# Splitting twelve unsplit float32 weight units: high part and negative by ScalarE, the rest by an adding transfer

## The chip, the cores and the metric

One core of a Trainium2 chip runs the kernel. The metric is the device time of one execution in microseconds; the median of several runs is what versions are compared by. Engines: PE (TensorE, matrix products; PEld are its weight loads), DVE (VectorE), ACT (ScalarE), POOL (GpSimd) and SP (SyncE, which here issues the loads). They run in parallel, each in the order of its own program, and wait for each other by semaphores.

## What is computed

Two transformer blocks in float32 on 256 tokens of width 1024. The first has sparse attention, retention and a gated feed-forward layer. The second has two layers, each of this form, and it is here that the change lies:

```python
h = rmsnorm(x, norm1_g[l])
u = h @ w_in[l]                       # q, k, v (512 each), 1024 for the convolution branch, 512 for the Fourier branch
y_a = differential_attention(q, k, v) @ w_proj_a[l]
cv = depthwise_conv(ga * sigmoid(gb), 31 taps) + conv_b[l]
y_b = silu(layernorm(cv)) @ w_proj_b[l]
y_c = fft2(four_in).real @ w_proj_c[l]
gates = sigmoid(h @ w_gate[l] + b_gate[l])      # three gates of 1024
merged = gates[0] * y_a + gates[1] * y_b + gates[2] * y_c
x = x + merged @ w_out[l]
x = x + (silu(f_gate) * f_up) @ w_ffn_out[l]    # f_gate, f_up = rmsnorm(x) @ w_ffn_in[l]
```

## The kernel before, in words

**Weights.** All weights come from HBM in 414 units, in the order of their use, each mostly 128 x 1024 float32 (512 KB). A unit is loaded by SP into one of `STAGE` = 5 staging buffers (`fetch`). For nearly all of them `split` then makes two parts in the reduced format float32r: ACT writes the high part `whi` (a conversion), DVE the low part `wlo` = weight - high part (`low`, one call later). There are `RING` = 8 buffers of each; a unit may be split when the unit eight before it is done. A product with a split weight is three products (`mm3`): high x high, high x low, low x high, as the activations are kept in two such parts too.

**The twelve others.** In each of the second block's layers the last two of the four units of the value projection (weight columns 1024 to 1535) and the last four of the eight units of the third gate (gate 2) are of the kind `WHOLE`. They are not split: PE multiplies the staged float32 weight with float32 activations (`self.whole`) in one float32 product each. Such a unit takes no slot of the ring, and keeps its staging buffer until its last product is done. `norm_steps(whole=True)` writes `self.whole` by four ACT copies at the end of the norm ahead of the layer (line 526).

**Ticks.** The program calls `tick` after each unit's products (for the projections of 512 columns after blocks of four or eight). A tick runs one step of every job that follows from the products just issued (jobs of priority 0: copies, gates, and the attention's steps), then `advance` (low parts, loads, and the split of one unit, or of two if under six units stand ready), then jobs of priority 1 to 3. The order of instructions on each engine is thus fixed when the program is written out.

**Order of a layer (`mix2`).** q, the convolution branch's inputs, k, the Fourier input, the value projection, gate 2, branch c, gate 0, gate 1, branch a (four units), branch b (four units), then w_out. Branch b multiplies the convolution's result, `slot[0]`.

**The convolution** (`convolve`, priority 3) is 124 DVE steps per layer (31 taps x 4 blocks) that are dealt out by credit, and `conv_norm` behind them, one stage for each tick: mean (PE) and subtraction (DVE); square (ACT); variance (PE), copy (DVE) and root (POOL); transposes (PE) and product (DVE); silu (ACT); high part (ACT); low part (DVE). Whatever is left of it is issued by `finish(conv)` right before branch b. `spent` is what an engine's instructions are planned to take:

```python
def vector_cost(name, out, args):
    return 0.065 + _width(args[0] if name == "tensor_reduce" else out) / 960
def tensor_cost(name, out, args):
    passes = 4 if args[0].dtype == F32 and name == "matmul" else 1
    return max(_width(out) * passes, 128) / 2400
...
while credit < 0.4 and not pace["last"]:
    mark = v.spent, t.spent
    yield
    credit += (t.spent - mark[1]) * pace["conv"] - (v.spent - mark[0])
credit -= 0.4
```

`pace["conv"]` is 1.0 from the value projection on.

Of the kernel before, what the change touches and what calls it, by code (L numbers as in the profile page):

```python
# [13 lines left out]
ALU = mybir.AluOpType  # L14
# [8 lines left out]
NF = FF // 128  # L23
LEAD_PAIRS = 2
CMP_AT = 9
WHOLE = 2
HEAD_ORDER = [g * 4 + p for p in range(4) for g in range(2)]


# [28 lines left out]
    return out + _pairs(w, FF)[2 * LEAD_PAIRS:]  # L58


WHOLES = {1024: 2, 0: 4}


def _whole(units, c):

    n = WHOLES.get(c, 0)
    return units[:len(units) - n] + [(t, WHOLE) for t, _ in units[len(units) - n:]]


def weight_units(a):  # L70
    out = []
    w = a["w_in"][0]
    heads = w[:, :512].reshape(D, 8, 64)[:, HEAD_ORDER].reshape(D, 512)
    kv = w[:, 512:1280].reshape(D, 6, 128)
    gates = w[:, 1280:1304].reshape(D, 8, 3)[:, HEAD_ORDER].reshape(D, 24)
    out += _token_major(np.concatenate([kv[:, 2], kv[:, 4], kv[:, 0], kv[:, 1]], 1))
    out += _token_major(heads)
    out += _token_major(np.concatenate([kv[:, 3], kv[:, 5], gates], 1))
    ret = [t for c in range(1304, 3352, 512) for t in _token_major(w[:, c:c + 512])]
    merge = _feature_major(w[:, 4376:6424])  # L80
    cmp = [(t, 1) for n in ("cmp_w1_k", "cmp_w1_v") for t, _ in _token_major(a[n][0], 4)]
    lin = out + ret
    out = []
    for i in range(len(lin)):
        out += lin[i:i + 1] + cmp[i - CMP_AT:i - CMP_AT + 1] * (CMP_AT <= i < CMP_AT + 8)
    out += merge[:8]
    for c in (3352, 3864):
        out += _token_major(w[:, c:c + 512])
    out += merge[8:]
    out += _feature_major(a["w_ret_branch"][0])  # L90
    out += _feature_major(a["w_nsa_branch"][0].reshape(8, 64, D)[HEAD_ORDER].reshape(512, D))
    out += _token_major(a["w_mix_out"][0], 1)
    out += _ffn_up(a["w_ffn_up"][0])
    out += _token_major(a["w_ffn_down"][0], 1)
    for l in range(2):
        w = a["w_in_2"][l]
        out += _token_major(w[:, :512])
        out += _pairs(w[:, 1536:2560], 512)
        for c in (512, 2560, 1024):
            out += _whole(_token_major(w[:, c:c + 512]), c)  # L100
        gate = [_feature_major(a["w_gate_2"][l][:, i * D:(i + 1) * D]) for i in range(3)]
        proj = [_feature_major(a[f"w_proj_{n}_2"][l]) for n in "abc"]
        out += _whole(gate[2], 0) + proj[2] + gate[0] + gate[1] + proj[0] + proj[1]
        out += _token_major(a["w_out_2"][l], 1)
        out += _ffn_up(a["w_ffn_in_2"][l])
        out += _token_major(a["w_ffn_out_2"][l], 1)
    return out
# [158 lines left out]
class Body:  # L266
# [3 lines left out]
    def __init__(self, ctx, tc, units, coff, poff, x, wts, cst, prm, rows, out):  # L270
        self.ctx, self.tc, self.nc = ctx, tc, Engines(tc.nc)
        self.units, self.coff, self.poff = units, coff, poff
        self.xin, self.wts, self.cst, self.prm, self.rows, self.out = x, wts, cst, prm, rows, out
        self.n = 0
        self.bg = []
        self.pending = None
        self.norming = None
        self.offs = np.concatenate([[0], np.cumsum([128 * u[0] for u in units])])
        self.fetched = self.split_to = 0
        self.look = self.STAGE  # L280
        self.raws, self.open, self.lows, self.held = {}, [], [], []
        self.ready, self.taken = ([], []), ([], [])

    def nm(self, s):
# [23 lines left out]
    def fetch(self):  # L308
        while (self.fetched < min(len(self.units), self.split_to + self.look)
               and (len(self.open) < self.STAGE or self.open[-self.STAGE][1])):  # L310
            i = self.fetched
            self.fetched += 1
            e = self.raws[i] = self.stage()
            w = self.units[i][0]
            self.nc.sync.dma_start(e[0][:, :w], bass.AP(tensor=self.wts.tensor,
                                                        offset=self.wts.offset + int(self.offs[i]), ap=[[w, 128], [1, w]]))

    def low(self):
        for hi, lo, e, w in self.lows:
# [4 lines left out]
    def split(self):  # L324
        i = self.split_to
        n = len(self.held)
        if i == len(self.units):
            return False
        w, kind = self.units[i]
        if kind != WHOLE and n >= self.RING and not self.held[n - self.RING][2]:  # L330
            return False
        self.fetch()
        if i not in self.raws:
            return False
        e = self.raws.pop(i)
        self.split_to += 1
        if kind == WHOLE:
            self.ready[0].append([e[0][:, :w], None, e])
            return True
        hi = self.t(self.wp, [128, 1024], "whi", F32R, bufs=self.RING)[:, :w]  # L340
        lo = self.t(self.wp, [128, 1024], "wlo", F32R, bufs=self.RING)[:, :w]
        self.nc.scalar.activation(hi, e[0][:, :w], AF.Copy)  # L342
        self.lows.append((hi, lo, e, w))
        u = [hi, lo, False]
        self.held.append(u)
        self.ready[kind].append(u)
        return True

    def advance(self):
        self.low()  # L350
        self.fetch()
        behind = sum(len(r) for r in self.ready) < 6 and self.norming is None
        for _ in range(2 if behind else 1):
            if not self.split():
                return

    def take(self, kind=0):
# [3 lines left out]
        u = self.ready[kind].pop(0)  # L361
        if any(x[0] is u[0] for x in self.lows):
            self.low()
        self.taken[kind].append(u)
        return u[:2]

    def done(self, n=1, kind=0):

        for _ in range(n):
            u = self.taken[kind].pop(0)  # L370
            if u[1] is None:
                u[2][1] = True
            u[2] = True


    def tick(self):
# [89 lines left out]
        return lambda: self.hi(hi[d], pv, scale), lambda: self.lo(hi[d], lo[d], pv, scale), pv  # L466


    def norm_steps(self, g_fin=None, whole=False):
        nc = self.nc  # L470
        stt, act = nc.vector.scalar_tensor_tensor, nc.scalar.activation
        if whole:
            self.whole = self.t(self.ap_, [128, KD, S], "act", bufs=4)
        acts = self.acts = self.act()
        rest = []
        g, pend = self.next_gain, self.pending
        es, rs = [None] * NT, {}
        half = [slice(i * 512, (i + 1) * 512) for i in range(2)]
# [42 lines left out]
                    stt(xs, xs, rs[tb][1][:, 0:1], g_fin[:, half[i]], op0=ALU.mult, op1=ALU.mult)  # L521

        def turn(tb, i):
            *fs, p = self.transpose4(es[tb][0], *acts, tb, 4 * i)
            if whole:
                rest.append(lambda: act(self.whole[:, 4 * i:4 * i + 4, tb * 128:tb * 128 + 128], p, AF.Copy))
            return fs

        add(0, 0)
        square(0, 0)  # L530
# [34 lines left out]
        for f in turn(1, 1):  # L565
            f()
        es[1][1] = True
        for f in rest:
            f()
        for tb in range(NT):  # L570
            final(tb)
        self.pending = None
# [9 lines left out]
    def lin_tok(self, n, consume, lead=False, tag="lin"):  # L582
# [4 lines left out]
        def block(todo):  # L587
            for i, (tb, k) in enumerate(todo):
                u = k // 2
                if u not in ws:  # L590
                    ws[u] = [w if w is None else w[:, :2 * n].rearrange("p (k n) -> p k n", k=2) for w in self.take()]
                wh, wl = ws[u]
                s = slice(tb * 128, (tb + 1) * 128)
                if wl is None:
                    self.nc.tensor.matmul(p[tb][:, :n], self.whole[:, k, s], wh[:, k % 2], start=k == 0, stop=k == KD - 1)
                else:
                    self.mm3(p[tb][:, :n], hi[:, k, s], lo[:, k, s], wh[:, k % 2], wl[:, k % 2], k == 0, k == KD - 1)
                if k == KD - 1:
                    consume(tb, p[tb][:, :n])
                if lead and i == 1 and (tb, k) == (0, 5):  # L600
# [19 lines left out]
    def lin_feat(self, acts, nk, groups, consume, start=0, tag="lin"):  # L620
        hi, lo = acts
        for g in range(start, groups):
            p = self.ps(tag).rearrange("p (f t) -> p f t", f=2)
            for f in range(2):
                if nk == KD or f == 0:
                    wh, wl = [w if w is None else w.rearrange("p (f k n) -> p f k n", k=nk, n=128) for w in self.take()]
                i = 0 if nk == KD else f
                for k in range(nk):
                    if wl is None:
                        self.nc.tensor.matmul(p[:, f], wh[:, i, k], self.whole[:, k], start=k == 0, stop=k == nk - 1)  # L630
                    else:
                        self.mm3(p[:, f], wh[:, i, k], wl[:, i, k], hi[:, k], lo[:, k], k == 0, k == nk - 1)
                if nk == KD or f == 1:
                    self.done()
                    if f == 1:
# [19 lines left out]
                    consume(g, ps)  # L655
                self.tick()

    def lin_res(self, acts, nk, g_fin=None, whole=False):
        hi, lo = acts
        final = self.next_gain is None  # L660
        cols = [[(0, 512), (512, 512)], [(0, 512), (512, 512)]]
# [37 lines left out]
                    self.tick()  # L699
            return  # L700
        self.pending = p
        self.norming = self.norm_steps(g_fin, whole)
        for tb in range(NT):
            for h in range(2):
                for kc in range(body, nk):
# [9 lines left out]
    def run(self):  # L715
# [65 lines left out]
        self.ffn(conv=True)  # L781
        for l in range(2):
            self.mix2(l)
            self.ffn(conv=False, whole=l == 0)

    def small_values(self):
        copy = self.nc.vector.tensor_copy
# [24 lines left out]
        yield  # L812


    def ffn(self, conv, whole=True):
        nc = self.nc
        stt, act = nc.vector.scalar_tensor_tensor, nc.scalar.activation
        with ExitStack() as ctx:
# [58 lines left out]
                self.lin_feat(self.acts, KD, NF, consume, start=LEAD_PAIRS, tag="s")  # L877
            else:
                self.lin_joint(self.acts, NF, consume_joint, start=LEAD_PAIRS)
            self.lin_res((hidh, hidl), NF, g_fin, whole)  # L880

    def lead_pairs(self, pool, consume):

# [876 lines left out]
```

## Time and profile before

| | |
|---|---|
| median of three runs | 1305.24 us (1305.23 to 1305.93) |
| the profiled execution | 1306.04 us |
| its span, first to last instruction | 1304.3 us |
| granted TensorE clock | 1.00 |
| PE busy | 1286.6 us (99%) |
| DVE, ACT, POOL busy | 923.2, 713.2, 68.9 us |
| loads and stores | 225.94 MB |

The profile is of one execution. Of its time 1.7 us lie around the span. Busy time is the union of an engine's instructions; the chain is the work that ended last, followed back from the last instruction to what released each step. Durations of single products are modelled to their ends, so the distance from one piece of the chain to the next is the better measure of what PE spends.

### The profile page before, as it was taken

What the parts mean: (1) busy time and instruction counts of PE and PEld (TensorE: products, weight loads), DVE (VectorE), ACT (ScalarE), POOL (GpSimd) and SP (SyncE); (2) the same over time, 40 slices, a digit from 0 to 9 for tenths busy, and PEclk for the clock granted to TensorE, in tenths of its full rate; (3) what the DMA queues carried; (4) which work ended last, traced back from release to release, by engine and by line L of the source; (5) the groups of instructions that cost most, each with busy time, mean ns of one, the idle gap of its engine ahead of it and who ended that gap; (6) DMA issues with size and microseconds to landing.
All of it is one profiled execution on the core that took longest, in us unless ns stands there. A gap on an engine that the chain in (4) does not pass through costs nothing.

```text
span 1304.3 us, 21120 instructions
## 1 busy us (share of the span) xinstructions
PE 1286.6 (99%) x8228; PEld 1149.1 (88%) x8228; DVE 923.2 (71%) x1521; ACT 713.2 (55%) x1259; POOL 68.9 (5%) x94
## 2 busy tenths in 40 slices
PE   6999999999999999999999999999999999999998
PEld 5878889999998879899998888888889999988887
DVE  5875555769887369998686766537989867766652
ACT  5664545457565364577455565436458664655540
POOL 0000000000000032100100000003100010000000
PEclk9999999999999999999999999999999999999999
DMA  8772235566566546245455655646525445565560
GB/s 294 263 239 97 82 129 184 186 195 201 176 191 208 163 139 216 99 146 172 155 178 190 196 182 188 205 142 199 188 74 183 159 145 178 195 193 188 183 195 33
DMA packets 63028, 225.94 MB, mean 173 GB/s; under 512 B 6992, under 2 KB 7376, under 8 KB 62928
## 3 DMA queue, kind: packets, MB, share of 16 engines
q1 hardware_dynamic: 62928, 224.60, 53.2%
q8 instruction: 64, 1.05, 0.3%
q14 instruction: 36, 0.29, 0.1%
HBM read 223.52 MB, written 1.05 MB: 172 GB/s over the span
## 4 chain that ended last, share of the span: by engine, by line
PE 95%; DVE 2%; DMA 1%; ACT 1%; issue 1%; POOL 0%; SPq 0%; POOLq 0%; ACTq 0%; DVEq 0%
PE lin L213 46%; PE s L213 38%; PE o L213 11%; DMA stage<-in_wts 1%; DVE wlo L213 0%; DVE stage L213 0%; DVE vr L213 0%; ACT whi L342 0%; DVE x L213 0%; ACT act L419 0%; POOL rs L503 0%; DVE prt L213 0%; POOL rs L506 0%; DVE act L213 0%; POOL rs L504 0%
## 5 line engine op out<-in xcount | busy, mean ns | idle before, releaser
L213 DVE TENSOR_TENSOR wlo<-stage,whi 128x1024 fp32r<-128x1024 f32 x402 | 479.5, 1215 | 109.9 <-ACT whi L342 109.6
L342 ACT ACTIVATE whi<-stage 128x1024 fp32r<-128x1024 f32 x402 | 412.4, 1053 | 132.3 <-PE o L213 57.9
L213 PE MATMUL s<-act,whi 128*128 128x256 f32 (+1 forms) x1600 | 367.0, 316 | 0.0
L213 PE MATMUL s<-act,wlo 128*128 128x256 f32 x1024 | 288.8, 282 | 0.0
L213 PEld LDWEIGHTS s<-act,whi 128*128 128x128 f32 x1600 | 263.9, 191 | 20.9
L213 PE MATMUL lin<-act,whi 128*128 128x256 f32 (+1 forms) x1344 | 281.9, 303 | 0.0
L213 PEld LDWEIGHTS lin<-act,whi 128*128 128x128 f32 x1344 | 215.5, 191 | 9.3
L213 PE MATMUL lin<-act,wlo 128*128 128x256 f32 x768 | 216.7, 282 | 0.0
L213 PE MATMUL lin<-whi,act 128*128 128x512 f32 (+2 forms) x736 | 213.8, 366 | 0.4 <-DVE prt L213 0.4
L213 PEld LDWEIGHTS s<-act,wlo 128*128 128x128 f32 x1024 | 195.2, 191 | 0.0
L213 PEld LDWEIGHTS lin<-whi,act 128*128 128x128 f32 x736 | 132.9, 190 | 21.9 <-DVE prt L213 0.8
L213 PEld LDWEIGHTS lin<-act,wlo 128*128 128x128 f32 x768 | 146.5, 191 | 0.0
L213 PE MATMUL lin<-wlo,act 128*128 128x512 f32 (+2 forms) x368 | 132.5, 360 | 0.3 <-DVE wlo L213 0.3
L213 DVE SCALAR_TENSOR_TENSOR cv<-gl,prm,cv 128x256 f32<-128x256 f32 x240 | 99.8, 477 | 0.0
L213 PEld LDWEIGHTS lin<-wlo,act 128*128 128x128 f32 x368 | 70.1, 190 | 10.2 <-DVE wlo L213 0.8
L832 ACT ACTIVATE y<-s 128x256 f32<-128x256 f32 x56 | 21.5, 383 | 64.6 <-PE s L213 64.6
L213 DVE SCALAR_TENSOR_TENSOR y<-s,prm,y 128x255 f32<-128x255 f32 x88 | 40.3, 480 | 16.9 <-ACT y L855 15.3
L213 PE MATMUL lin<-wlo,hidh 128*128 128x512 f32 x132 | 52.2, 395 | 0.0
L213 PE MATMUL lin<-whi,hidl 128*128 128x512 f32 x132 | 52.2, 395 | 0.0
L213 PE MATMUL lin<-whi,hidh 128*128 128x512 f32 x132 | 52.0, 394 | 0.0
L213 PE MATMUL o<-whi,hidh 128*128 128x512 f32 (+1 forms) x132 | 49.8, 377 | 0.0
L213 PE MATMUL o<-wlo,hidh 128*128 128x512 f32 (+1 forms) x132 | 49.6, 376 | 0.0
(285 smaller groups left out, 1558.4 us busy)
## 6 DMA issues: line engine op xcount, KB each, us to landing
stage<-in_wts SPq DMA_DIRECT2D x410, 512.0 KB, 4.2
gbc<-in_rows SPq DMA_DIRECT2D x7, 512.0 KB, 4.4
stage<-in_wts SPq DMA_DIRECT2D x4, 280.0 KB, 4.0
x<-in_x SPq DMA_DIRECT2D x4, 256.0 KB, 5.3
on<-in_cst SPq DMA_DIRECT2D x1, 896.0 KB, 7.0
out_dram<-x SPq DMA_DIRECT2D x3, 256.0 KB, 2.0
cst<-in_cst SPq DMA_DIRECT2D x1, 514.5 KB, 5.2
gbc<-in_rows SPq DMA_DIRECT2D x2, 256.0 KB, 6.4
```

The lines of the kernel that those rows point to most:

```text
L213: return f(out, *args, **kw)
L342: self.nc.scalar.activation(hi, e[0][:, :w], AF.Copy)
L832: act(sg[0][:, f], ps[f][:, 1], AF.Copy)
```

## The change

The twelve units get the kind `SUMMED` in place of `WHOLE`. ACT writes the high part as for every unit, and also the negative of it, by a second conversion of the staged weight with scale -1, into the buffer of the low part. The staging buffer is free after that. At the next `advance` POOL issues a transfer that reads the unit's weights from HBM again and adds them onto that buffer, which then holds weight - high part. DVE has no part in it. The products become `mm3`, the units take slots of the ring, and the unsplit activations with their four copies go.

```diff
+    def add_up(self):
+
+        for lo, i in self.sums:
+            self.nc.gpsimd.dma_start(out=lo, in_=self.unit(i), accum_op=ALU.add)
+        self.sums = []
...
-        if kind != WHOLE and n >= self.RING and not self.held[n - self.RING][2]:
+        if n >= self.RING and not self.held[n - self.RING][2]:
             return False
...
-        if kind == WHOLE:
-            self.ready[0].append([e[0][:, :w], None, e])
-            return True
         hi = self.t(self.wp, [128, 1024], "whi", F32R, bufs=self.RING)[:, :w]
         lo = self.t(self.wp, [128, 1024], "wlo", F32R, bufs=self.RING)[:, :w]
         self.nc.scalar.activation(hi, e[0][:, :w], AF.Copy)
-        self.lows.append((hi, lo, e, w))
+        if kind == SUMMED:
+            self.nc.scalar.activation(lo, e[0][:, :w], AF.Copy, scale=-1.0)
+            e[1] = True
+            self.sums.append((lo, i))
+            kind = 0
+        else:
+            self.lows.append((hi, lo, e, w))
...
     def advance(self):
+        self.add_up()
         self.low()
...
+        if any(x[0] is u[1] for x in self.sums):
+            self.add_up()
...
         def turn(tb, i):
-            *fs, p = self.transpose4(es[tb][0], *acts, tb, 4 * i)
-            if whole:
-                rest.append(lambda: act(self.whole[:, 4 * i:4 * i + 4, tb * 128:tb * 128 + 128], p, AF.Copy))
-            return fs
+            return self.transpose4(es[tb][0], *acts, tb, 4 * i)[:2]
...
-                if wl is None:
-                    self.nc.tensor.matmul(p[tb][:, :n], self.whole[:, k, s], wh[:, k % 2], start=k == 0, stop=k == KD - 1)
-                else:
-                    self.mm3(p[tb][:, :n], hi[:, k, s], lo[:, k, s], wh[:, k % 2], wl[:, k % 2], k == 0, k == KD - 1)
+                self.mm3(p[tb][:, :n], hi[:, k, s], lo[:, k, s], wh[:, k % 2], wl[:, k % 2], k == 0, k == KD - 1)
```

`lin_feat` loses its `wl is None` branch in the same way.

## Rows read from the trace of the kernel before

**Rows 1.** The page, parts 1 and 4: busy times, chain by engine.

```profile
PE 1286.6 (99%) x8228; PEld 1149.1 (88%) x8228; DVE 923.2 (71%) x1521; ACT 713.2 (55%) x1259; POOL 68.9 (5%) x94
...
PE 95%; DVE 2%; DMA 1%; ACT 1%; issue 1%; POOL 0%; SPq 0%; POOLq 0%; ACTq 0%; DVEq 0%
```

**Rows 2.** One stretch, busy: us, PE, PEld, DVE, ACT, POOL; PEclk; DMA.

```profile
500.00:533.00 33.00, 33.00 (x167) 28.00 (x166) 32.48 (x65) 13.88 (x20) 7.85 (x4) 1.00 0.64 206
```

**Rows 3.** Groups on PE by shape: count, busy us, mean ns.

```profile
L213 PE MATMUL lin<-act,stage 128*128 128x256 f32 x128 | 29.2, 381 | 0.0
```

**Rows 4.** The chain, 500 to 600: start us, us, what.

```profile
505.10 27.37 PE lin L213 x120
...
533.33 3.43 PE lin L213 x8
...
559.74 3.46 PE lin L213 x16
...
564.58 3.52 PE lin L213 x16
...
578.30 2.88 PE lin L213 x24
...
582.55 2.94 PE lin L213 x24
```

**Rows 5.** Timeline of ACT, 464 to 486: start us, us, what.

```profile
477.13 2.07 ACT L526 ACTIVATE act<-s 128x512 f32<-128x512 f32 x4
```

**Rows 6.** The tile stage: ns min/median/max; loads to landing.

```profile
L342 ACT ACTIVATE whi<-stage x402: 652/1054/1127, 9.2 to 1278.5; 128x1024 fp32r<-128x1024 f32 x133, 128x560 fp32r<-128x560 f32 x1
...
DMA to landing us min/median/max: 2.8/4.2/8.2
```

**Rows 7.** Timeline of POOL, 640 to 650.

```profile
645.26 1.16 POOL L436 TENSOR_SCALAR rsc<-rsc 128x2 f32<-128x2 f32 x1 [13.87 <-DVE rsc L213]
646.51 0.70 POOL L437 TENSOR_TENSOR rsc<-rsc,mhalf 128x2 f32<-128x2 f32 x1
```

**Rows 8.** DVE's convolution steps in three stretches: span, busy us, count.

```profile
584.00:607.00 23.00, 0.00 (x0) 1.00 0.56 182
607.00:635.00 28.00, 11.42 (x27) 1.00 0.49 155
...
1023.00:1051.00 28.00, 11.43 (x27) 1.00 0.49 153
```

**Rows 9.** The chain in order of time, 600 to 690.

```profile
635.39 1.95 PE s L213 x10
...
643.29 1.68 PE s L213 x16
...
647.95 0.22 PE s L213 x2
648.17 14.38 PE lin L213 x120
662.55 11.52 PE s L213 x96
```

**Rows 10.** Timeline of DVE, 630 to 666.

```profile
645.01 0.16 DVE L213 COPY rsc<-s 128x2 f32<-128x2 f32 x1 [1.29 <-PE s L213]
...
648.20 1.22 DVE L213 TENSOR_TENSOR cv<-cv,s 128x1024 f32<-128x1024 f32 x1 [1.83 <-PE s L213]
...
653.95 0.69 DVE L213 SCALAR_TENSOR_TENSOR tg<-tg,lin 128x512 f32<-128x512 f32 x1 [3.39 <-PE lin L213]
...
655.28 1.22 DVE L213 TENSOR_TENSOR wlo<-stage,whi 128x1024 fp32r<-128x1024 f32 x1
...
659.30 1.29 DVE L213 TENSOR_TENSOR act<-cv,act 128x512 fp32r<-128x512 f32 x2
```

**Rows 11.** Timeline of ACT, 630 to 666.

```profile
654.17 2.08 ACT L1449 ACTIVATE cv<-cv,prm 128x256 f32<-128x256 f32 x4
...
657.11 1.14 ACT L419 ACTIVATE act<-cv 128x512 fp32r<-128x512 f32 x2
```

More of the change, by code (lines that the diff above doesn't have):

```diff
@@ L25 @@
 CMP_AT = 9
-WHOLE = 2
+SUMMED = 2
 HEAD_ORDER = [g * 4 + p for p in range(4) for g in range(2)]
@@ L58, in _ffn_up, with _summed @@
     return out + _pairs(w, FF)[2 * LEAD_PAIRS:]
[L61 to L67, printed above, removed]
+SUMS = {1024: 2, 0: 4}
+def _summed(units, c):
+    n = SUMS.get(c, 0)
+    return units[:len(units) - n] + [(t, SUMMED) for t, _ in units[len(units) - n:]]
 def weight_units(a):
@@ L99, in weight_units @@
         for c in (512, 2560, 1024):
-            out += _whole(_token_major(w[:, c:c + 512]), c)
+            out += _summed(_token_major(w[:, c:c + 512]), c)
         gate = [_feature_major(a["w_gate_2"][l][:, i * D:(i + 1) * D]) for i in range(3)]
         proj = [_feature_major(a[f"w_proj_{n}_2"][l]) for n in "abc"]
-        out += _whole(gate[2], 0) + proj[2] + gate[0] + gate[1] + proj[0] + proj[1]
+        out += _summed(gate[2], 0) + proj[2] + gate[0] + gate[1] + proj[0] + proj[1]
         out += _token_major(a["w_out_2"][l], 1)
@@ L280, in __init__ @@
         self.look = self.STAGE
-        self.raws, self.open, self.lows, self.held = {}, [], [], []
+        self.raws, self.open, self.lows, self.held, self.sums = {}, [], [], [], []
         self.ready, self.taken = ([], []), ([], [])
@@ L314, in fetch, with unit @@
             w = self.units[i][0]
-            self.nc.sync.dma_start(e[0][:, :w], bass.AP(tensor=self.wts.tensor,
-                                                        offset=self.wts.offset + int(self.offs[i]), ap=[[w, 128], [1, w]]))
+            self.nc.sync.dma_start(e[0][:, :w], self.unit(i))
+    def unit(self, i):
+        w = self.units[i][0]
+        return bass.AP(tensor=self.wts.tensor, offset=self.wts.offset + int(self.offs[i]), ap=[[w, 128], [1, w]])
+    def add_up(self):
+        for lo, i in self.sums:
+            self.nc.gpsimd.dma_start(out=lo, in_=self.unit(i), accum_op=ALU.add)
+        self.sums = []
     def low(self):
@@ L369, in done @@
         for _ in range(n):
[L370 to L373, printed above, removed]
+            self.taken[kind].pop(0)[2] = True
     def tick(self):
@@ L466, in transpose4, with norm_steps @@
         return lambda: self.hi(hi[d], pv, scale), lambda: self.lo(hi[d], lo[d], pv, scale), pv
-    def norm_steps(self, g_fin=None, whole=False):
+    def norm_steps(self, g_fin=None):
         nc = self.nc
         stt, act = nc.vector.scalar_tensor_tensor, nc.scalar.activation
-        if whole:
-            self.whole = self.t(self.ap_, [128, KD, S], "act", bufs=4)
         acts = self.acts = self.act()
-        rest = []
         g, pend = self.next_gain, self.pending
@@ L523, in turn @@
         def turn(tb, i):
-            *fs, p = self.transpose4(es[tb][0], *acts, tb, 4 * i)
-            if whole:
-                rest.append(lambda: act(self.whole[:, 4 * i:4 * i + 4, tb * 128:tb * 128 + 128], p, AF.Copy))
-            return fs
+            return self.transpose4(es[tb][0], *acts, tb, 4 * i)[:2]
         add(0, 0)
@@ L567, in norm_steps @@
         es[1][1] = True
-        for f in rest:
-            f()
         for tb in range(NT):
@@ L590, in block @@
                 if u not in ws:
-                    ws[u] = [w if w is None else w[:, :2 * n].rearrange("p (k n) -> p k n", k=2) for w in self.take()]
+                    ws[u] = [w[:, :2 * n].rearrange("p (k n) -> p k n", k=2) for w in self.take()]
                 wh, wl = ws[u]
                 s = slice(tb * 128, (tb + 1) * 128)
-                if wl is None:
-                    self.nc.tensor.matmul(p[tb][:, :n], self.whole[:, k, s], wh[:, k % 2], start=k == 0, stop=k == KD - 1)
-                else:
-                    self.mm3(p[tb][:, :n], hi[:, k, s], lo[:, k, s], wh[:, k % 2], wl[:, k % 2], k == 0, k == KD - 1)
+                self.mm3(p[tb][:, :n], hi[:, k, s], lo[:, k, s], wh[:, k % 2], wl[:, k % 2], k == 0, k == KD - 1)
                 if k == KD - 1:
@@ L625, in lin_feat @@
                 if nk == KD or f == 0:
-                    wh, wl = [w if w is None else w.rearrange("p (f k n) -> p f k n", k=nk, n=128) for w in self.take()]
+                    wh, wl = [w.rearrange("p (f k n) -> p f k n", k=nk, n=128) for w in self.take()]
                 i = 0 if nk == KD else f
                 for k in range(nk):
[L629 to L632, printed above, removed]
+                    self.mm3(p[:, f], wh[:, i, k], wl[:, i, k], hi[:, k], lo[:, k], k == 0, k == nk - 1)
                 if nk == KD or f == 1:
@@ L656, in lin_joint, with lin_res @@
                 self.tick()
-    def lin_res(self, acts, nk, g_fin=None, whole=False):
+    def lin_res(self, acts, nk, g_fin=None):
         hi, lo = acts
@@ L701, in lin_res @@
         self.pending = p
-        self.norming = self.norm_steps(g_fin, whole)
+        self.norming = self.norm_steps(g_fin)
         for tb in range(NT):
@@ L783, in run @@
             self.mix2(l)
-            self.ffn(conv=False, whole=l == 0)
+            self.ffn(conv=False)
     def small_values(self):
@@ L812, in layer_values, with ffn @@
         yield
-    def ffn(self, conv, whole=True):
+    def ffn(self, conv):
         nc = self.nc
@@ L879, in ffn @@
                 self.lin_joint(self.acts, NF, consume_joint, start=LEAD_PAIRS)
-            self.lin_res((hidh, hidl), NF, g_fin, whole)
+            self.lin_res((hidh, hidl), NF, g_fin)
     def lead_pairs(self, pool, consume):
```

## The prediction

> **What bounds the kernel now.** I read the busy times first, then the chain that ended last, then the busy times of stretches, then the chain piece by piece. TensorE (PE) is busy for 1286.6 of 1304.3 us and holds 95% of the chain [rows 1]; in the stretch in which the first of the twelve units would be split it is busy 33.00 of 33.00 us at granted clock 1.00 [rows 2], which is its upper level. So time is won only where PE's own work shrinks, and lost wherever PE is made to wait. VectorE (DVE) is nearly full there too, 32.48 of 33, ScalarE (ACT) is not, 13.88, and GpSimd (POOL) hardly works.
>
> **The PE term.** A float32 product shows as two records (64 products of the gate units, 128 records, [rows 3]), so a float32 gate unit of eight products is a piece of 16 and a float32 unit of the value projection a piece of 8. In the chain the gate pieces take 3.46 and 3.52 us in turn; the next units of that size, already split into three products each, are pieces of 24 and take 2.88 and 2.94 us [rows 4]. Of the value projection's units a float32 one takes 3.43 us, and ten split ones before it 27.37, or 2.74 each. Per layer: 2 x (3.43 - 2.74) = 1.38, and 2 x (3.46 + 3.52 - 2.88 - 2.94) = 2.32, together 3.70 us. Both layers: 7.4 us less PE work. These are forms the kernel already runs, so I take the term as nearly certain.
>
> **ACT.** Removed: four copies into the unsplit activations at each layer's start, 2.07 us [rows 5]. PE does not wait for them. Added: two conversions for each of 12 units at 1.05 us [rows 6], 25 us in all, in stretches where ACT is idle more than half of the time [rows 2], and six units ahead of the use; I cost both at nothing. Without that cover a unit would hold PE for about 2.1 us, 25 us in all.
>
> **The adding transfers.** No row shows one. A unit is split while six others stand ready, so six units of at least 2.74 us, some 16 us, lie between its split and its first product. Of these go one tick (2.9 us) until the transfer is issued and about 2.1 us of ACT; 11 us are left. A plain load of the same 512 KB lands in 4.2 us, at most 8.2 [rows 6]; POOL's nearest instructions take 0.7 to 1.2 us [rows 7]. From below the price is nothing, from above each us past the 11 costs 12 us over the kernel. I take nothing, since the longest load plus the longer POOL row, 9.4 us, still fits. What is queued behind a transfer on POOL is the root of the q and k norms and of the convolution's norm; by program order the former is issued in ticks before the first transfer, the latter long after the last. The SP queue gets no new work, and the other loads come earlier, as float32 units no longer hold staging buffers until their last product; nothing waits for those today.
>
> **Ring and staging.** The 12 units now take ring slots. By the code's rule (a slot is free when the unit eight back is done) the float32 units and those between them are split between one tick later and three ticks earlier than today, and at the end of gate 2 as many units are split in both kernels; PE sees no difference.
>
> **What is late next: the convolution.** This is where I differ from the plain sum. The convolution's steps are put into DVE's queue by credit: each tick adds PE's planned time, less DVE's planned other work, and a step costs 0.4. A float32 product is planned at four passes, 4 x 512/2400 = 0.853 us or 0.427; three split ones at 0.64 or 0.32. Eight products of the value projection and 32 of gate 2 per layer lose 1.71 and 3.41, so 5.12 us of credit, 13 steps. The trace shows how thin the credit is: no step at all in 584 to 607, then 27 steps in 28 us, in both layers [rows 8]. In the ticks at the end a tick of 24 products of 256 columns gives 2.56, a weight's low part takes 0.065 + 1024/960 = 1.13, and in two of the next four ticks another step 0.33: 1.20 + 1.20 + 1.43 + 1.43 = 5.26, just over what was lost. With three ticks, 3.83, the steps would not be through; a fifth is needed only if 0.3 more were lost. So the convolution ends four ticks later against PE.
>
> Today its last step falls into the tick of gate 1's third unit; the mean's products follow after the fourth (the piece of 10 at 635.39), the variance's after the sixth (1.68 us at 643.29), the transposes after the seventh (647.95), then silu, high part and low part in the ticks of the eighth, a1 and a2 [rows 9]. Calling a1 to a4 the units of branch a and b1 the first of branch b: the low part ends 659.30 + 1.29 = 660.59 [rows 10], b1 starts at 662.55 [rows 9]. The reserve is two ticks. Four ticks later, mean after gate 1's eighth unit, variance after a2, transposes after a3, silu in a4's tick, and the high and low parts are flushed right before b1, which reads them.
>
> With zero at the end of a2: PE does the variance to 1.7 and a3 (14.38/5 = 2.88) to 4.6. DVE first does branch a's two steps on a2, 655.28 - 653.95 = 1.33, and a weight's low part, 1.2, then the copy, 0.16: 2.7. POOL takes 1.95 (645.26 to 647.21, [rows 7]): 4.75. The transposes wait 0.25, and a4 ends at 7.9. DVE does the same steps for a3 from 4.6 to 7.1, then the 1.22 us product: 8.3. ACT's four silus, 2.08, end at 10.5, the first half of the high part (half of 1.14, and latency) at 11.1 [rows 11]; the low part, 0.69 for a half, at 11.85. b1's second product needs it and would have run at 8.0: 3.8 us. With the 0.25 a layer loses 4.1 us. Bounds of the tail: 1.8 us if DVE took the norm's steps ahead of branch a's and the weights' (the transposes then end at 4.8, and 1.22 + 2.08 + 0.6 + 0.69 behind them at 9.5, against 7.8; the order of emission gives no reason for it), 4.8 if PE waited for both halves of both parts (1.14 + 1.29 in place of half of them).
>
> **Sum.** 1306.04 - 7.4 + 2 x 4.1 = 1306.7 for the profiled execution, whose span is 1304.3 with 1.7 around it. It stands 0.8 above the runs' median, 1305.24, so the median should be 1305.9. A transfer queue on POOL may add to what lies around the span; no row bounds it except that 1.7, and I take nothing.
>
> **Rivals.**
> 1. The saving stands: the norm's tail hides, since the convolution's end moves by two ticks or fewer or its steps go ahead of branch a's. For it speaks DVE's and ACT's free time in this stretch (ACT starts silu 4.75 us after its input is ready today, 649.42 to 654.17, so it has room); against it, that the order is fixed by the program and branch a's steps stand ahead. 1305.24 - 7.4 = 1297.8; with the lower bound of the tail, 1.8, 1301.4.
> 2. The adding transfer comes late (slower): its place is each float32 unit's first product, its price what it lands past 11 us after the split's conversions; it decides from 0.16 us on, since 12 x 0.16 and the forecast's 0.7 make 2.6. One us late on each: 1305.9 + 12 = 1318. For it: a transfer that reads, adds and writes must do more than a load, and 8.2 us occurs even for loads. Against: DMA queues were busy 0.64 of the time at most there [rows 2].
> 3. The tail is longer: PE waits for the whole tile, 4.8 us and more, or the mean's products wait for DVE at gate 1's end as DVE works off 13 steps more: 5.5 us a layer, 1305.24 - 7.4 + 11 = 1308.8.
>
> On rival 2 the Trainium skill has a rule, page "SBUF — State Buffer", section "Who interferes with whom": a transfer issued from GpSimd has its descriptors written by GpSimd, which is locked out while VectorE runs a copy, cast or tensor_scalar in a two-port mode; tensor_tensor is not among them. In the trace DVE is all but full in the stretch where these transfers would be issued, though with the convolution's scalar_tensor_tensor and the weights' tensor_tensor; if the rule held for all of DVE's work, the time would be rival 2's, otherwise the forecast's.
>
> **Chances.** The forecast (tail of 2.5 to 5.0 us a layer) 0.60; rival 1 0.20; rival 2 0.08; rival 3 0.12. The measurement tells a change from none at about 0.2%, 2.6 us. The forecast alone spans 1303 to 1307.8. The range reaches down to 1300, which takes in rival 1 at the tail's lower bound but not the whole saving (about 0.13 left out), and up to 1309.5, which takes in rival 3 and leaves out rival 2 (0.07). Faster by over 0.2%: rival 1, 0.20. Same: 0.60. Slower: rivals 2 and 3, 0.20.
>
> **What would show it.** The pieces of 16 at gate 2 become pieces of 24 of 2.9 us. In the chain an entry of ACT or DVE (silu, high or low part of the convolution) appears before branch b in each layer, PE waits there 3.5 to 4.5 us, and the mean's products stand right before branch a. At the float32 units' places PE waits for no transfer. Wrong if PE waits for the low parts of weights, if branch b starts without a wait, or if the mean's products still stand before gate 1's fifth unit.

## The result and the profile after

The changed kernel takes 1316.38 us (median of four runs, 1315.22 to 1317.02) against 1305.55 us for the kernel before, timed beside it. The ratio is 1.0082, interval [1.0070, 1.0093]: slower by 10.8 us, and outside the predicted range of 1300.0 to 1309.5.

The profiled execution took 1315.22 us, with a span of 1313.3 us. The page's parts 1, 4 and 6 of the changed kernel, against [rows 1] and the loads of [rows 6]:

```profile
PE 1286.0 (98%) x8308; PEld 1154.5 (88%) x8308; DVE 923.7 (70%) x1521; ACT 730.8 (56%) x1275; POOL 79.5 (6%) x106
...
PE 91%; DVE 4%; ACT 2%; issue 1%; DMA 1%; POOL 0%; SPq 0%; ACTq 0%; DVEq 0%; POOLq 0%
...
stage<-in_wts SPq DMA_DIRECT2D x410, 512.0 KB, 4.1
wlo<-in_wts POOLq DMA_DIRECT2D x12, 512.0 KB, 7.9
```

PE is busy for only 0.6 us less, although the twelve units alone take 7.3 us less (e8, below); its idle time grew by 9.6 us, from 17.7 to 27.3, and its share of the chain fell from 95% to 91%. PE's waits, as the view of waits sums them over the whole kernel (what waited, for whom: us in total, times, longest):

```profile
PE s L213 <- ACT act L431: 6.6, 2, 3.3
PE s L213 <- ACT pr L1540: 1.4, 2, 0.7
PE o L213 <- ACT wT L1565: 0.9, 2, 0.4
PE s L213 <- DVE qs L213: 0.5, 2, 0.3
```

None of these four stands in the kernel before, where PE has no wait over 1.4 us after the first 11 us. There is none for a transfer. The tile view of `wlo` has the time from issue to landing of the twelve:

```profile
DMA to landing us min/median/max: 5.5/7.9/11.2
```

**The tail.** The chain in order of time, 640 to 715 us, in the first of the two layers (start, us, what); before it was [rows 9]:

```profile
645.37 1.73 PE s L213 x8
647.09 5.75 PE lin L213 x48
652.84 1.68 PE s L213 x16
654.52 2.99 PE lin L213 x24
658.87 1.22 DVE wlo L213
660.08 1.14 DVE cv L213
661.25 2.08 ACT cv L1447 x4
663.33 0.53 ACT act L431
...
663.88 0.70 DVE act L213
...
664.63 13.93 PE s L213 x95
```

The mean's products (the piece of 8 at 645.37) now stand behind gate 1's eighth unit, the variance's behind a2, and branch b waits for what hangs behind them: a weight's low part on DVE, the convolution's product, four silus, then the high and the low part. Branch b itself takes 13.93 us in place of 11.52, with the same products. The reason is in the windows of this stretch (busy: us, PE, PEld, DVE, ACT, POOL; granted clock; DMA share; GB/s):

```profile
655.00:660.00 5.00, 5.00 (x44) 5.00 (x44) 2.93 (x6) 2.34 (x2) 0.89 (x2) 1.00 0.34 125
660.00:665.00 5.00, 1.53 (x7) 1.03 (x7) 4.76 (x7) 3.75 (x7) 0.00 (x0) 0.80 0.35 113
665.00:670.00 5.00, 5.00 (x26) 5.00 (x26) 0.23 (x2) 0.32 (x1) 0.00 (x0) 0.52 0.26 100
670.00:675.00 5.00, 5.00 (x44) 5.00 (x43) 4.59 (x6) 2.30 (x4) 0.00 (x0) 1.00 0.28 84
```

From the wait of 3.3 us on, the granted clock is half for a while, 1.2 in place of 2.4 GHz: PE is busy throughout 665 to 670, yet starts 26 products where it starts 44 five microseconds later.

**The attention.** ACT's order of work, 540 to 553 us (start, us, instruction; in brackets the idle time ahead of it):

```profile
540.44 1.05 ACT L348 ACTIVATE whi<-stage 128x1024 fp32r<-128x1024 f32 x1
541.38 1.05 ACT L350 ACTIVATE wlo<-stage 128x1024 fp32r<-128x1024 f32 x1
542.33 0.37 ACT L1655 ACTIVATE u<-o 128x256 f32<-128x256 f32 x1
544.74 0.38 ACT L1661 ACTIVATE u<-o 128x256 f32<-128x256 f32 x1 [2.03 <-DVE mg L213]
545.02 1.05 ACT L348 ACTIVATE whi<-stage 128x1024 fp32r<-128x1024 f32 x1
545.97 1.05 ACT L350 ACTIVATE wlo<-stage 128x1024 fp32r<-128x1024 f32 x1
546.91 0.58 ACT L1514 ACTIVATE qT<-s 96x512 fp32r<-96x512 f32 x1
547.39 0.59 ACT L1514 ACTIVATE kT<-s 96x512 fp32r<-96x512 f32 x1
...
549.29 0.47 ACT L1540 ACTIVATE pr<-s,nm 128x256 f32<-128x256 f32 x1
```

The negatives (L350) stand in ACT's queue ahead of the copies and exponentials from which attention's small products are made (qT, kT, pr). ACT has idle time here too (2.03 us), but it lies ahead of an instruction that waits, not where the queue is long.

**The balance.** The starts of three of PE's instructions cut each layer into stretches: the first Fourier product, the last product of attention with its values, the first low-part product of branch b, the first product of w_out. Against before, in us:

| stretch | layer 0 | layer 1 |
|---|---|---|
| Fourier products to attention's end | -0.92 | -1.11 |
| from there to branch b | +4.34 | +4.18 |
| branch b | +2.10 | +1.49 |

They sum to +10.08; all that precedes the layers was 1.05 us shorter in this execution, which makes the 9.0 us between the two spans. The forecast was -3.70, +4.1 and 0 in each layer. In the first stretch the listed waits make only 1.4 us a layer of what is missing against -3.70; the granted clock is 1.00 in all of it, and the rest stands as longer busy time of PE, whose ends are modelled. That part was not taken apart.

### The profile page after: what moved, and what is told of

Same layout as the page of the kernel before. It is cut to its first block, busy times and chain, and to the rows that moved or that the text cites. A ratio compares the mean times of both kernels' runs of the same rounds, so it can differ in the third digit from the quotient of the medians.

```text
span 1313.3 us, 21344 instructions
## 1 busy us (share of the span) xinstructions
PE 1286.0 (98%) x8308; PEld 1154.5 (88%) x8308; DVE 923.7 (70%) x1521; ACT 730.8 (56%) x1275; POOL 79.5 (6%) x106
## 3 DMA queue, kind: packets, MB, share of 16 engines
HBM read 229.81 MB, written 1.05 MB: 176 GB/s over the span
## 4 chain that ended last, share of the span: by engine, by line
PE 91%; DVE 4%; ACT 2%; issue 1%; DMA 1%; POOL 0%; SPq 0%; ACTq 0%; DVEq 0%; POOLq 0%
PE lin L213 43%; PE s L213 37%; PE o L213 11%; DVE cv L213 1%; DMA stage<-in_wts 1%; DVE wlo L213 1%; ACT pr L1540 1%; DVE stage L213 0%; ACT whi L348 0%; DVE vr L213 0%; ACT cv L1447 0%; ACT act L431 0%; DVE act L213 0%; ACT qs L1504 0%; DVE x L213 0%
## 5 line engine op out<-in xcount | busy, mean ns | idle before, releaser
L348 ACT ACTIVATE whi<-stage 128x1024 fp32r<-128x1024 f32 x414 | 425.6, 1053 | 134.4 <-PE o L213 60.2
L213 PE MATMUL s<-act,whi 128*128 128x256 f32 (+1 forms) x1600 | 371.5, 318 | 7.1 <-ACT act L431 6.6
L213 PE MATMUL lin<-act,whi 128*128 128x256 f32 (+1 forms) x1472 | 306.1, 301 | 0.0
L213 PEld LDWEIGHTS s<-act,whi 128*128 128x128 f32 x1600 | 267.2, 193 | 28.9 <-ACT act L431 7.1
L213 PEld LDWEIGHTS lin<-act,whi 128*128 128x128 f32 x1472 | 235.3, 191 | 9.3
L213 PE MATMUL lin<-act,wlo 128*128 128x256 f32 x832 | 234.8, 282 | 0.0
L213 PE MATMUL lin<-whi,act 128*128 128x512 f32 (+2 forms) x768 | 224.4, 367 | 0.4 <-DVE prt L213 0.4
L213 PEld LDWEIGHTS lin<-whi,act 128*128 128x128 f32 x768 | 138.6, 190 | 22.9 <-DVE prt L213 0.8
L213 PEld LDWEIGHTS lin<-act,wlo 128*128 128x128 f32 x832 | 158.7, 191 | 0.0
L213 PE MATMUL lin<-wlo,act 128*128 128x512 f32 (+2 forms) x384 | 138.8, 361 | 0.6 <-DVE wlo L213 0.6
```

What stands on the lines that cost most here:

```text
L213: return f(out, *args, **kw)
```

## The experiments

### The tail by itself: e1, e2

The first kernel is the changed one with a planner that still books each of the twelve units at four passes:

```diff
+        summed = kind == SUMMED
+        if summed:
...
-        u = [hi, lo, False]
+        u = [hi, lo, False, summed]
...
+        if u[3]:
+            self.nc.tensor.spent += 4 * 512 / 2400
```

> The changed kernel, but the planner still counts the twelve units' products at four passes, so the convolution's steps stand in the same ticks as before the change. Theory (the convolution's tail costs 4 us a layer, and the wait drops TensorE's clock, 2.4 and 1.2 us): no wait and no clock loss at branch b, 1316.4 - 8.1 - 3.6 = 1304.7, up to 1307 if the attention's waits grow because VectorE has more to do there. Rival (the time was lost to the adding transfers or to ScalarE's second conversions all along): within 2 us of 1316.

1304.71 us against 1305.43, ratio 0.9995 [0.9986, 1.0004]. The wait at branch b is gone in both layers and the clock stays at 1.00 there.

The second is the kernel before, with that credit taken away and nothing else:

```diff
         if u[1] is None:
+            self.nc.tensor.spent -= 4 * 512 / 2400
```

> The kernel before, with one thing changed: the planner counts the products of the twelve float32 units at three passes in place of four. Theory: the convolution ends four ticks later, TensorE waits about 4 us at branch b in each layer and its clock falls behind that wait, 1305.5 + 8.1 + 3.6 = 1317. Rival (the clock falls because of the new transfers or the denser products): the waits come, the clock stays at 1.00, 1313.6.

1317.74 us, ratio 1.0098 [1.0083, 1.0113]. PE's waits in it:

```profile
PE s L213 <- ACT act L421: 6.6, 2, 3.3
```

Its clock behind the wait of layer 0 (a window, busy as above):

```profile
668.00:671.00 3.00, 3.00 (x16) 3.00 (x15) 0.00 (x0) 0.00 (x0) 0.00 (x0) 0.50 0.00 0
```

So a number in the planner, which adds and removes no instruction and only changes their order, costs 12.3 us: 4.34 and 4.33 up to branch b, 2.27 and 2.43 in it. This shows the tail's cause, and that the clock belongs to it.

### The second conversions and the transfers: e3, e4

e3 leaves out the negative, and the transfer writes in place of adding; e4 leaves out the transfer alone.

```diff
-            self.nc.gpsimd.dma_start(out=lo, in_=self.unit(i), accum_op=ALU.add)
+            self.nc.gpsimd.dma_start(out=lo, in_=self.unit(i))
...
-            self.nc.scalar.activation(lo, e[0][:, :w], AF.Copy, scale=-1.0)
```

> The changed kernel without ScalarE's second conversion; GpSimd's transfer writes the weights in place of adding them, so the low part of the twelve units holds the whole weight. Theory (the second conversions make ScalarE late in the value projection and gate 2, and the attention's products wait 2.8 us a layer): these waits go, 1316.4 - 5.6 = 1310.8, with the tail's waits as they are. Rival (TensorE got faster than the attention's chain of VectorE and ScalarE, whatever the conversions): 1315 to 1316.5.

1312.52 us, ratio 1.0059 [1.0042, 1.0076], 3.9 below the changed kernel. The first stretch of the layers is now 3.03 and 3.00 us shorter than before, close to the 3.70 forecast; the tail is as it was (4.34, 4.33). Of the attention's waits for ACT one is left:

```profile
PE o L213 <- ACT wT L1564: 0.8, 2, 0.4
```

The run changes two things at once: a transfer that only writes lands sooner than the adding ones did (7.9 us):

```profile
wlo<-in_wts POOLq DMA_DIRECT2D x12, 512.0 KB, 5.3
```

e4 tells the two apart.

```diff
-            self.nc.gpsimd.dma_start(out=lo, in_=self.unit(i), accum_op=ALU.add)
+            pass
```

> The changed kernel without GpSimd's adding transfers; the low part of the twelve units stays the negative of the weight. Theory (the transfers are hidden): 1315 to 1317, waits at the same places. Rival (the transfers slow the loads or hold GpSimd, and the attention's waits are theirs): 1310.8 or less.

1315.38 us, ratio 1.0080 [1.0065, 1.0095]. The median is 1.0 us below the changed kernel's and the span of the profiled execution 0.7: that is the most that the twelve transfers can be given. In the first stretch of the layers it is 0.2 over both: without them these are 1.13 and 1.12 us shorter than before, with them 0.92 and 1.11. So the 4.0 us that e3 wins there are not the transfers', whether they add or write, but the negatives'. The waits for ACT (act 6.6, pr 1.4, wT 0.9) are unchanged without them. Rival 2, whose time was the nearest to the result, is not what happened. One reason to fear it was the Trainium skill, page "SBUF — State Buffer", section "Who interferes with whom", by which copies, casts and tensor_scalar in two-port modes on VectorE can lock GpSimd out. No run here shows GpSimd locked out: in the changed kernel the transfers took POOL 0.87 us each to issue (median; at most 1.21), and landed. But DVE, busy for 26.7 us of the 30 from 520 to 550, did hardly any of the operations that the rule names (two copies of 128x2), so these runs agree with it and do not put it to the test.

### The tail cured otherwise: e5, e6

Both restore the credit by the factor `pace`, from gate 0 on, behind the attention; e6 has e3's edit too.

```diff
-            pace["conv"] = 1.0
+            pace["conv"] = 1.17
```

> The changed kernel with the convolution's pace raised from 1.0 to 1.17 from gate 0 on, so that the lost credit comes back behind the attention's dense stretch and the last step stands in the tick it had before the change. Theory: the tail's wait and the clock's fall go, the waits of the value projection and gate 2 (some 3 us a layer, from ScalarE's second conversions) stay: 1316.4 - 8.1 - 3.6 = 1304.7, 1303 to 1306. Rival (VectorE can't take the steps there and TensorE waits for weights' low parts in gate 0 and gate 1): over 1308.

1306.66 us against 1305.63, ratio 1.0006 [0.9997, 1.0015]: the wait at branch b goes, but not all of the tail. The mean's products now wait 0.8 us for ACT, and the transposes ahead of them 0.2 for DVE; the stretch up to branch b is 1.49 and 1.47 us longer than before, at a granted clock of 1.00.

> The same, and without ScalarE's second conversion: GpSimd's transfer writes the weights instead of adding them, so the low part of the twelve units holds the whole weight. If the tail, the clock and the second conversion are the three things that took the gain, what is left is TensorE's saving less about 1 us a layer: 1305.4 - 7.4 + 2 = 1300, 1299 to 1301.5. Rival (something else takes most of it): over 1303.

1302.19 us, ratio 0.9975 [0.9964, 0.9985]. That is a little above the expected 1299 to 1301.5: the 1.5 us a layer up to branch b are left. The negatives are worth 4.5 us in this pair, 3.9 between the changed kernel and e3.

### Another engine for the negatives: e7, e8

e7 is e5 with the negative written by POOL.

```diff
-            self.nc.scalar.activation(lo, e[0][:, :w], AF.Copy, scale=-1.0)
+            self.nc.gpsimd.tensor_scalar(lo, e[0][:, :w], -1.0, None, op0=ALU.mult)
```

> As the first, but GpSimd writes the negative in place of ScalarE, and then issues its transfer. Theory: as without the conversion if GpSimd's 128x1024 operation is done in time, 1300 to 1302. Rival (GpSimd's operation is slow or holds VectorE off, and low parts come late): 1304.7 or more.

1318.85 us, ratio 1.0105 [1.0089, 1.0120]. POOL's groups by shape (count | busy us, mean ns of one | idle before):

```profile
L350 POOL TENSOR_SCALAR wlo<-stage 128x1024 fp32r<-128x1024 f32 x12 | 36.1, 3006 | 10.0 <-DMA stage<-in_wts 5.6 <-PE lin L213 4.5
```

PE's waits:

```profile
PE lin L213 <- DMA wlo<-in_wts: 8.4, 3, 5.5
PE o L213 <- ACT u L1661: 2.5, 2, 1.2
```

At 3.0 us each the negatives queue with the norms' roots on POOL, the transfers are issued late, and here PE does wait for them, 5.5 us in layer 0 and 2.5 in layer 1. The rival of the expectation came true. The granted clock, in two stretches of layer 0 and in the one of layer 1 that holds the wait of 2.5 us:

```profile
535.00:541.00 6.00, 0.79 (x4) 0.32 (x2) 6.00 (x9) 1.33 (x2) 4.48 (x3) 0.99 1.03 283
541.00:546.00 5.00, 4.75 (x23) 4.01 (x24) 4.92 (x12) 2.22 (x4) 2.92 (x2) 0.67 1.04 340
...
960.00:965.00 5.00, 3.16 (x22) 2.79 (x22) 5.00 (x11) 1.71 (x3) 4.59 (x3) 1.00 1.04 376
```

e8 splits the twelve units as all others are, with DVE's low part and no transfer, at a pace of 1.4:

```diff
-        if kind == SUMMED:
-            self.nc.scalar.activation(lo, e[0][:, :w], AF.Copy, scale=-1.0)
-            e[1] = True
-            self.sums.append((lo, i))
-            kind = 0
-        else:
-            self.lows.append((hi, lo, e, w))
+        self.lows.append((hi, lo, e, w))
+        kind = 0 if kind == SUMMED else kind
...
-            pace["conv"] = 1.0
+            pace["conv"] = 1.4
```

> The twelve units split as all others, the low part by VectorE, with no second conversion and no transfer; the convolution's pace is 1.4 from gate 0 on, which puts its last step near the tick it had before the change. Theory (ScalarE's second conversions made the attention late): ScalarE is relieved as in the run without them, VectorE gets 6.9 us more a layer, of which the stretch up to gate 2 has to take most: 1300 to 1304. Rival (VectorE is the one that is full there): 1306 or more.

1314.82 us, ratio 1.0068 [1.0055, 1.0081]. The first stretch gets 3.64 and 3.63 us shorter, and PE has no wait in it. That is the PE term to within 0.07 us, with the twelve high parts still on ACT: these cost nothing here. More than the negatives differs, though: there is no transfer, DVE writes the twelve low parts, and the pace is 1.4 from gate 0 on. The convolution's steps then crowd the gates, and the transposes of attention's output wait:

```profile
PE s L213 <- DVE ao L213: 10.7, 2, 5.3
```

With that wait too the clock is half, as two windows of layer 0 show:

```profile
630.00:636.00 6.00, 0.67 (x6) 0.46 (x4) 5.52 (x14) 0.00 (x0) 2.88 (x2) 0.86 0.46 158
636.00:641.00 5.00, 4.93 (x14) 3.66 (x15) 4.06 (x7) 2.94 (x6) 0.00 (x0) 0.50 0.31 105
```

### Credit kept, and the two kinds of units apart: e9, e11, e12

e9 is e1 without the negatives (the edits of e1 and e3 together).

> The changed kernel with both causes taken away in the other way: the planner counts the twelve units at four passes, as before the change, and ScalarE makes no second conversion (GpSimd's transfer writes the weights, so the low part of the twelve units holds the whole weight). Theory (saving 3.6 us a layer, less 0.6 for what is left of the attention's waits, no tail, no clock loss): 1305.4 - 6.0 = 1299.4, up to 1301 as VectorE has more steps in that stretch. Rival (the steps in the dense stretch cost as much as the tail did, whatever ScalarE does): 1304 or more.

1301.15 us against 1305.26, ratio 0.9970 [0.9958, 0.9982]: 3.6 below e1, just over the upper end of what was expected. In three settings, then, the twelve negatives are worth 3.6, 3.9 and 4.5 us, in each with the adds turned into plain writes, which e4 bounds.

e11 and e12 have e1's bookkeeping, and split only the value projection's two units of a layer (e11) or only gate 2's four (e12); the rest stay unsplit as before.

```diff
-    return units[:len(units) - n] + [(t, SUMMED) for t, _ in units[len(units) - n:]]
+    kind = SUMMED if c in (1024,) else WHOLE
+    return units[:len(units) - n] + [(t, kind) for t, _ in units[len(units) - n:]]
```

(In e12 the condition reads `c in (0,)`.)

> Only the value projection's two units of each layer are split with the adding transfer, gate 2's four stay float32; the planner counts four passes as before. Their second conversions fall into ticks where ScalarE has little to do. Theory: the saving of these units, 1.2 us a layer, stands: 1305.4 - 2.4 = 1303.0. Rival (their transfers or conversions cost as much): 1305 or more.

1303.91 us, ratio 0.9989 [0.9981, 0.9998], 1.4 us faster than before. These units are split ahead of the attention's small steps, and PE waits 0.2 us between 530 and 600. Of the kernels that compute the whole reference it is the only one whose interval lies below 1.

> The other half: only gate 2's four units of each layer are split with the adding transfer, the value projection's two stay float32; four passes counted. Theory (their conversions, in the ticks in which the attention begins, are the costly ones): a saving of 2.4 us a layer less waits of 2 to 3: 1304.5 to 1306.5. Rival (the conversions of the value projection's units are the costly ones): 1301.

1311.19 us, ratio 1.0048 [1.0035, 1.0060], 4.7 us above the highest that was expected. The first stretch is 2.55 and 2.57 us longer than before. What stands out is ACT's order, from its timeline:

```profile
546.95 1.06 ACT L352 ACTIVATE whi<-stage 128x1024 fp32r<-128x1024 f32 x1
547.89 1.05 ACT L355 ACTIVATE wlo<-stage 128x1024 fp32r<-128x1024 f32 x1
548.84 1.05 ACT L352 ACTIVATE whi<-stage 128x1024 fp32r<-128x1024 f32 x1
549.79 1.05 ACT L355 ACTIVATE wlo<-stage 128x1024 fp32r<-128x1024 f32 x1
550.74 0.58 ACT L1539 ACTIVATE qT<-s 96x512 fp32r<-96x512 f32 x1
```

PE's waits between 540 and 600 us:

```profile
PE s L214 <- ACT kT L1539: 2.0, 2, 1.8
PE s L214 <- DVE qs L214: 0.8, 1, 0.8
```

Four conversions in a row stand before qT, where the changed kernel has two. By the code, the unsplit units ahead of them hold no slots of the ring, so two units can be split in one tick; that reading was not tested by itself. The mean granted clock of the kernel stays at 1.00.

### Two more ACT instructions in the kernel before: e10

The kernel before, with each staged float32 weight negated twice in place (which leaves it as it was):

```diff
         if kind == WHOLE:
+            for _ in range(2):
+                self.nc.scalar.activation(e[0][:, :w], e[0][:, :w], AF.Copy, scale=-1.0)
```

> The kernel before, with two ScalarE operations of 128x1024 on each of the twelve float32 units (the staged weight negated twice in place), at the ticks where they are staged. Theory (ScalarE's work there makes the attention late even with the slower products): 1 to 2 us a layer, 1307.5 to 1309.5. Rival (only the faster products make the attention's chain the limit): 1305 to 1306.

1315.12 us, ratio 1.0076 [1.0062, 1.0090]; the direction was right, the size was 9.9 us where 2 to 4 were expected. PE's waits:

```profile
PE s L213 <- ACT kT L1518: 3.2, 4, 1.0
PE lin L213 <- ACT kn L1478: 2.1, 2, 1.1
PE s L213 <- DVE qs L213: 1.6, 2, 0.8
```

No split, no transfer and no credit differ here, only 24 short ACT instructions, 25 us of work on an engine that is busy 55% of the time. More than a third of that comes out as time. Here, too, four of them stand in a row right before qT:

```profile
547.68 4.18 ACT L339 ACTIVATE stage<-stage 128x1024 f32<-128x1024 f32 x4
```

## Why the prediction was wrong, point by point

- **The PE term** (3.70 us a layer): right. The first stretch got 3.64 and 3.63 us shorter in e8, and 3.0 in e3 and e6.
- **ACT** ("I cost both at nothing"): this step failed. The forecast priced ACT's added work by its idle share in a stretch [rows 2] and by the six units between a split and its use, that is, by when the weights are needed. For these PE never waited. What was late stood behind the conversions in ACT's queue: qT, kT, qs, pr and wT, each on a chain of short hops between PE, ACT and DVE. The prediction named what stood behind the transfers on POOL, but not what stood behind the conversions on ACT. Taking the negatives out brings 3.6 to 4.5 us in three pairs, and adding 24 conversions of that length to the kernel before costs 9.9. The first stretches missed the -7.27 that e8 shows to be there by 5.24 us; leaving the negatives out (e3) brings back 2.11 and 1.89 of it. Of the other 1.2 us the adding transfers are 0.2 (e4); a wait of 0.8 for ACT's wT stays in e3 and is gone in e8, and why was not taken apart.
- **The adding transfers** (nothing): right to within 1.0 us. They land in 7.9 us (median), inside the 11 that were allowed, but the longest took 11.2 and there is little to spare: in e5 and e11 PE waits once, 0.3 and 0.2 us, for a transfer. The forecast's bound, the longest plain load and a POOL row, 9.4 us, was too low. Issuing costs POOL 0.87 us. Where the transfers do come late (e7), PE waits as rival 2 said.
- **Ring and staging** ("PE sees no difference"): e12 points to a way in which the ring could matter through ACT: which slots are free decides how many conversions stand in a row. This is read from the code and from ACT's order, and in the changed kernel itself it was not separated from the negatives.
- **The convolution's credit and the tail** (four ticks, 4.1 us a layer): right in place, order and nearly in size. The mean stands right before branch a, the wait is for silu and the high part, and PE stands still for 3.3 us and 0.1 to 0.3 us behind it, where 3.5 to 4.5 were forecast. e2 gives it alone, e1 takes it away. Some of it is luck. The four ticks rest on a sum with a slip: 2.56 - 1.13 - 0.33 is 1.10 and not 1.20, so four ticks give 5.06, just short of the 5.12 that were lost, and by its own rule a fifth tick would have been needed. And its 0.25 us for the transposes did not come: POOL's root took 0.97 us (655.59 to 656.56) in place of 1.95.
- **The clock**: missing from the sum. The two stretches of the tail grew by 6.44 and 5.67 us; 3.47 and 3.66 of these are waits, which leaves 2.97 and 2.01 us for the same products in windows of half clock, 5.0 us over the kernel. The forecast had a wait of this length in it and priced only the wait. The trace of the kernel before could not have given the price, as no wait of PE is over 1.4 us in it after the first 11 us; the clock's loss could have been named as a rival, and was not.

In short, -7.27 for the products, +5.24 for ACT's queue and what was not separated from it, +7.1 for the two waits and +5.0 for the clock make the +10.08. The forecast had the first and third of these terms. Two steps failed, then: ACT's added work at nothing, and the clock, which no term held. Rival 2 named nearly the right time by a cause that was not there.

What stays open is the best arrangement. With the credit kept (e1, e9) DVE does more of the convolution inside the attention (79 of its steps in the first stretch of layer 0 with e1, where the changed kernel has 66, 13 fewer, as was forecast): e9 still waits 0.5 us a layer for DVE there, and its first stretches are 1.42 and 2.41 us shorter, where e3's, with less credit, are 3.0. A planner that gives credit early for the tail and keeps steps late for the attention was not tried beyond e5 and e6.

## What to carry to other kernels

An engine that is idle half of the time is no cover for added work: look at what stands behind the new instruction in its queue, and whether PE waits on a chain of short steps through that queue. Where a planner spends PE's planned time, a change to what a product is booked at moves work elsewhere; price that as a change of its own, and test it alone, as e2 did. When a forecast contains a wait on PE, look up in the rows what the clock did behind waits of that length, and add it; where no row has such a wait, name the clock's loss as a rival of its own.

## What the runs showed of the hardware

- With PE waits of 3.3 us (changed kernel, e2, e3, e4) and of 5.3 to 5.5 us (e7, e8) the granted clock went to half for some microseconds. With waits of 1.8 us (e12) and 2.5 us (e7, layer 1) it stayed at 1.00.
- An adding transfer of 512 KB, issued by POOL, landed in 7.9 us (median of 12); one that only wrote, from the same queue, in 5.3 (e3); a plain load of that size, issued by SP, in 4.1. The Trainium skill, page "DMA: Bandwidth & Descriptors", section "Anatomy of one DMA — SWDGE (gpsimd) path", gives 2.0 us plus the bytes over 436e3; by that this size would take an estimated 3.2 us, which neither of POOL's two kinds reached here, and the measured times stand.
- The negation of a 128x1024 weight took ACT 1.05 us and POOL 3.0 us (mean of 12).
